# Product of probabilities and values once for four query tiles in forgetting attention and once for two in dilated attention, with pools split by stage

## The chip, the core and the metric

The kernel runs on one core of one Trainium2 chip. The metric is the device time of one execution in microseconds (us). The core has five engines that run at the same time, each through a stream of its own in order: TensorE (PE; its weight loads are listed as PEld), VectorE (DVE), ScalarE (ACT), GpSimd (POOL) and SyncE (SP), which issues the DMAs. TensorE writes to PSUM, which is cut into banks of 512 fp32 columns; the other engines copy from there to SBUF.

## The reference

Two blocks, one after the other, on 1024 tokens of 1024 channels, all in fp32. The first runs a state space model (SSD) and forgetting attention with 16 heads side by side, and merges them; the second runs differential attention with 4 heads and dilated attention with 8, and a gated embedding. The two attentions that the change touches, cut down:

```python
def forgetting_attention(q, k, v, logf):      # 16 heads of 64, 16 + 1024 keys
    c = cumsum(logf)
    for each block of 128 queries i:
        s = q_i @ k.T * scale + (c_i - c_k)
        s = where(kpos <= qpos, s, -inf)      # causal
        p = softmax(s)
        o_i = p @ v

def dilated_attention(q, k, v, slopes):       # 8 heads of 64, three patterns
    for window, dilation in ((128, 1), (512, 4), (2048, 16)):
        # query t sees t + j * dilation, |j| <= window // (2 * dilation)
        o, lse = banded softmax(q @ k.T * scale - slope * distance) @ v
    out = sum(softmax(lse) * o)
```

## The kernel before

All work is written out in one order by hand; no scheduler changes it. A stage is a Python generator that gives back the TensorE time which it has just used by its own estimate, and `merge(a, b, ratio)` takes steps from two of them in turn, so that projections (fp32 split into a high and a low part, three matmuls each, `mm3`, L112 to L114) stand between the steps of an attention. In forgetting attention these steps are also those of the convolution and of the next pair's projections.

Heads go in pairs of two, p = 0 to 7 in forgetting attention, n = 4 to 7 in dilated attention. A pair's 1024 queries are 8 tiles of 128, and `pipeline` (L526) runs three stages over them, the scores two tiles ahead: for tile i the order is A(i+2), C(i-1), B(i).

- A: scores of a tile for both heads (L566, L567, L569 forgetting, L1262 and L1264 dilated) into PSUM; VectorE adds the bias and takes the minimum (L570, L1267; four such reductions for a dilated tile); ScalarE takes the exponential (L573, L1270) into `N`.
- B: the probabilities are transposed on TensorE, 128 x 128 at a time (L620, L1289, L1295), and copied from PSUM to `pt` (L626 on ScalarE in forgetting attention; VectorE and ScalarE in turn in the dilated). In the dilated one 3 x 16 more keys of each head are first gathered by VectorE into `more` (L1285) and transposed by L1296.
- C: the product with the values, 64 output rows per head, both heads in one bank O (L599; L1313). Each is a matmul of 128 query columns, once per block of keys. In forgetting attention L604 adds the first 16 keys of four tiles at once, in the dilated one L1314 adds the `more` keys of a tile.

After every fourth tile O is read out (L606 on VectorE; L1317 on ScalarE). In pairs 4 to 6 of the dilated attention projections of the next pair stand between the steps, with the sums of squares of q and k (L255, transposed by tokens at L264) and a reciprocal root on VectorE (L239 to L246), whose rows are transposed by L271. The last pair, n = 7, has no such work beside it.

Tiles come from a pool `big` of 41 slots (N, pt, projections, weights), from small pools, and from `ph`, which holds what one phase needs (`cb`, `pm`, `E`, the tables). A tile is free again when its last reader is through, and what writes to it next waits for that.

Of the kernel before, what the change touches and what calls it, by code (L numbers as in the profile page):

```python
# [57 lines left out]
# steps of a pair's projections, for the first pair, the differential and the dilated ones: t the tail of the attention  # L58
# before it, f and e what is left to finish of the pairs before it, q, v and z the projections of q, v and the gate,
# N the norms of k and q, x the values by tokens  # L60
# [6 lines left out]
class Kern:  # L67
    def __init__(self, ctx, tc, t, out):
        self.tc, self.nc, self.t, self.out = tc, tc.nc, t, out
        self.big = ctx.enter_context(tc.tile_pool(name="big", bufs=41))  # L70
        self.cst = ctx.enter_context(tc.tile_pool(name="cst", bufs=1))
        self.sm = ctx.enter_context(tc.tile_pool(name="sm", bufs=2))
        self.dr = ctx.enter_context(tc.tile_pool(name="dr", bufs=1, space=bass.MemoryType.DRAM))
        self.ctx, self.psx = ctx, None
        self.psum(8, 0)
        self.n = 0
        self.halfs = None

# [5 lines left out]
    def half(self, name):  # L84
        """512 columns; in the tail from a pool of their own"""
        if self.halfs is None:
            return self.slot(name, w=512)
        return self.halfs.tile([128, 512], F32, tag="half", name=name, bufs=11)

    def psum(self, one, two):  # L90
        """the banks of PSUM from here on: single ones and pairs"""
# [40 lines left out]
    # weight strips, in the order in which they are used  # L132
# [85 lines left out]
    def rstd(self, out, ss, n):  # L218
        """1 / sqrt(ss / n + eps)"""
# [9 lines left out]
    def rsqrt(self, v, pool):  # L229
        """v [128, n] > 0 in place to 1/sqrt(v): a first guess from the exponent, three Newton steps"""  # L230
# [29 lines left out]
    def token_sums_T(self, t, n):  # L260
        """the sums by tokens: [128 tokens, block of 128, part, 32]"""
# [5 lines left out]
    def rows_out(self, v, n, dst):  # L267
        """v [128 tokens, n = (row, block of 128)]: rows of 1024 tokens in DRAM"""
# [56 lines left out]
    def softplus(self, x):  # L325
        """x [128, 9, n] in place to max(x, 0) + log(1 + exp(-|x|)), the logarithm by the series of artanh"""
# [16 lines left out]
    def dt_f(self):  # L343
# [21 lines left out]
        # cumulative log forget gates (negated: csp), as rows  # L365
# [31 lines left out]
    def dt_ssd(self):  # L397
        """SSD: within-chunk cumulative a*dt, decays"""
# [61 lines left out]
    def v_tokens(self, vT, blocks):  # L460
        """vT [128 channels, tokens] -> [128 tokens, block, 128 channels]"""
# [54 lines left out]
    def silu2(self, ps, out):  # L516
        """2 * silu"""
# [5 lines left out]
    def pipeline(n, A, B, C, pre=lambda i: None):  # L523
        """stages of each of n query tiles, the scores two tiles ahead"""
# [13 lines left out]
    def fox_attend(self, p, st):  # L538
# [10 lines left out]
        Ns, PTs, O, M = {}, {}, [None], [None, None]  # L549
# [30 lines left out]
        def B(i):  # L580
            PTs[i] = []
            if i % 4 == 3:
                ps = self.bank()
                te.transpose(ps[:, :128], M[i // 4][:, 0], self.ident)
                nc.vector.tensor_copy(out=M[i // 4][:, 1], in_=ps[:, :128])
            for j in range(2):
                pt = self.slot("pt", w=1024)
                self.transposes(Ns[i][j], 16, i + 1, pt, act=True)
                PTs[i].append(pt)
# [3 lines left out]
        def C(i):  # L593
            if i % 4 == 0:
                O[0] = self.bank()
            for b in range(i + 1):
                for j in range(2):
                    o = O[0][64 * j:64 * j + 64, (i % 4) * 128:(i % 4 + 1) * 128]
                    te.matmul(o, st["v"][:, b, 64 * j:64 * j + 64], PTs[i][j][:, b * 128:(b + 1) * 128],  # L599
                              start=i % 4 == 0 and b == 0, stop=False)  # L600
            del PTs[i]
            if i % 4 == 3:
                for t in range(4):
                    te.matmul(O[0][:, t * 128:(t + 1) * 128], st["vm"][:, t], M[i // 4][:, 1], start=False, stop=t == 3)  # L604
                c = slice((i - 3) * 128, (i + 1) * 128)
                nc.vector.scalar_tensor_tensor(out=y[:, c], in0=O[0], scalar=0.5, in1=st["zs"][:, c], op0=ALU.mult,  # L606
                                               op1=ALU.mult)
            return (i + 1) * 269
# [4 lines left out]
    def transposes(self, N, off, nb, pt, act=False):  # L613
        nc = self.nc
        for g in range(0, nb, 4):
# [5 lines left out]
            self.evac(pt[:, g * 128:(g + n) * 128], ps[:, :n * 128], act)  # L621
# [9 lines left out]
    def conv_strip(self, j):  # L631
        """strip j of xbc: projection, causal convolution, silu; channel-major, all 1040 tokens"""
# [24 lines left out]
    def ssd_chunks(self, g, st):  # L657
# [9 lines left out]
        def tokens(c, c0, w):  # L667
            """x*dt, decayed x*dt and B by tokens"""
# [32 lines left out]
        def prep(c):  # L701
# [9 lines left out]
            E = self.ph.tile([128, 520], F32, tag="cb", name="E", bufs=2)  # L711
# [61 lines left out]
    def ssd_gate(self, g, st):  # L773
        """y * silu(z), the group's sum of squares, out to DRAM"""
# [14 lines left out]
    def ssd_ssq(self, g, st):  # L789
        """1/rms of the group, as a row in DRAM"""  # L790
# [18 lines left out]
    def inv_rows(self, n, dst):  # L809
        """1/l of n heads, as rows in DRAM"""  # L810
# [6 lines left out]
    def gates(self, ms):  # L817
        """tanh(half the gate's argument), out to DRAM"""
# [10 lines left out]
    def load_y(self, g):  # L829
        """four row blocks of the attention's (g < 2) or the SSD's output, hi and lo; the loads run ahead"""  # L830
# [41 lines left out]
    def merge_out(self, ys, late):  # L872
        nc, V, G, t = self.nc, self.nc.vector, self.nc.gpsimd, self.t
        A = [self.slot("A", w=T) for _ in range(8)]
# [95 lines left out]
    def wide_product(self, w, act, wo, begun=(), before=None):  # L970
        """token-major products of act (channel-major halves) with w [1024, 1024]; yields
        (half, token tile of the half, column half, psum); begun: the first sums"""
# [21 lines left out]
    def wide_rows(self, w, ch, out, pool=False, vector=False):  # L994
        """the row blocks of w [K, 1024], columns ch*512.., hi and lo, into out"""
# [13 lines left out]
    def qk_norms(self, parts, dst):  # L1009
        """parts: k and q, each (x, x squared, gain); x * gain / rms of each head of 64; dst: two rows in DRAM  # L1010
        for each"""
# [19 lines left out]
    def raw_project(self, key, st):  # L1031
        """a strip of two heads, and its squares"""
# [769 lines left out]
```

## Time and profile before

| | |
|---|---|
| Time, median of 3 runs | 2734.22 us (2733.99 to 2737.39) |
| Span of the profiled execution | 2737.4 us, as long as the highest time |
| TensorE, matmuls | 2670.8 us busy, 98% |
| VectorE | 1377.0 us, 50% |
| ScalarE | 1171.9 us, 43% |
| GpSimd | 685.0 us, 25% |
| Mean granted clock of TensorE | 0.994 |

The profile is of one execution. Forgetting attention runs from 97 to 682 us, the SSD and the merge after it, the dilated pairs from about 2215 to 2523 us. An engine's busy time is what its instructions took; where an engine was idle, the row names what ended the wait. A matmul's end is modelled, so what a matmul costs is read from the start of one to the start of the next.

### The profile page before, as it was taken

How to read it: one execution, taken by the hardware profiler on the slowest of the kernel's cores; microseconds unless marked ns; L12 is line 12 of the kernel's file. 1: busy time of each engine (PE TensorE's matmuls, PEld its weight loads, DVE VectorE, ACT ScalarE, POOL GpSimd, SP SyncE). 2: the span in 40 equal slices, each digit the busy share in tenths (PEclk: the TensorE clock that was granted, in tenths of full speed). 3: DMA queues.
4: the chain of work that ended last, by engine and by line, in shares of the span. 5: the costliest groups of instructions: out<-in, count | busy, mean ns of one | idle time of the engine just before them, and what ended most of it. 6: DMA issues, size and time to landing. Idle time of an engine off the chain costs nothing. (4 is left out here: it accounts for less than half of the span.)

```text
span 2737.4 us, 40266 instructions
## 1 busy us (share of the span) xinstructions
PE 2670.8 (98%) x15693; PEld 2264.5 (83%) x15693; DVE 1377.0 (50%) x2761; ACT 1171.9 (43%) x2080; POOL 685.0 (25%) x764
## 2 busy tenths in 40 slices
PE   8999999999999999999999999999999999998999
PEld 6888888889989989889887887877878877787887
DVE  5433222333474574664756777445644555446332
ACT  5444444454343443434432113445544554445331
POOL 1111111111244243342433334111111121114321
PEclk9999999999999999999999999999999999999999
DMA  3212222211123123122157654340222223324422
GB/s 124 65 57 78 71 78 78 78 47 47 70 83 118 47 85 116 49 84 108 62 186 253 215 185 161 108 130 26 85 62 78 79 79 97 98 72 138 166 67 70
DMA packets 85471, 266.98 MB, mean 98 GB/s; under 512 B 10880, under 2 KB 12032, under 8 KB 84256
## 3 DMA queue, kind: packets, MB, share of 16 engines
q1 hardware_dynamic: 85280, 264.40, 29.9%
q8 instruction: 123, 2.02, 0.3%
q14 instruction: 68, 0.56, 0.1%
HBM read 205.57 MB, written 33.49 MB: 87 GB/s over the span
## 5 line engine op out<-in xcount | busy, mean ns | idle before, releaser
L121 POOL TENSOR_TENSOR wlo<-wraw,whi 128x1024 fp32r<-128x1024 f32 (+2 forms) x168 | 374.3, 2231 | 1279.5 <-ACT whi L120 1242.6
L112 PE MATMUL bank<-uh,whi 128*128 128x512 f32 (+4 forms) x1752 | 628.4, 359 | 0.1
L114 PE MATMUL bank<-uh,wlo 128*128 128x512 f32 (+4 forms) x1752 | 619.7, 354 | 0.4 <-POOL wlo L121 0.4
L113 PE MATMUL bank<-ul,whi 128*128 128x512 f32 (+4 forms) x1752 | 619.5, 354 | 0.0
L112 PEld LDWEIGHTS bank<-uh,whi 128*128 128x128 f32 (+1 forms) x1752 | 328.9, 188 | 36.4 <-issue 3.5
L114 PEld LDWEIGHTS bank<-uh,wlo 128*128 128x128 f32 (+1 forms) x1752 | 328.6, 188 | 35.9 <-POOL wlo L121 0.9
L113 PEld LDWEIGHTS bank<-ul,whi 128*128 128x128 f32 (+1 forms) x1752 | 328.9, 188 | 32.2
L112 PE MATMUL bank<-u,whi 128*128 128x512 f32 x512 | 207.6, 405 | 0.7 <-ACT pr L931 0.7
L113 PE MATMUL bank<-u,whi 128*128 128x512 f32 x512 | 203.5, 397 | 0.0
L114 PE MATMUL bank<-u,wlo 128*128 128x512 f32 x512 | 203.2, 397 | 0.0
L120 ACT ACTIVATE whi<-wraw 128x1024 fp32r<-128x1024 f32 (+2 forms) x169 | 155.6, 927 | 24.3 <-DMA wraw<-in_w_pa_dram 15.1
L626 ACT ACTIVATE pt<-bank 128x512 f32<-128x512 f32 (+1 forms) x320 | 143.4, 507 | 37.2 <-PE bank L620 28.0
L114 PE MATMUL bank<-yh,wlo 128*128 128x512 f32 x384 | 153.0, 399 | 2.0 <-POOL wlo L121 1.9
L112 PE MATMUL bank<-yh,whi 128*128 128x512 f32 x384 | 152.8, 398 | 1.0 <-ACT whi L120 1.0
L113 PE MATMUL bank<-yl,whi 128*128 128x512 f32 x384 | 152.1, 396 | 0.0
L643 DVE SCALAR_TENSOR_TENSOR acc<-raw,cwh,acc 128x1040 f32<-128x1040 f32 x72 | 93.7, 1302 | 114.0 <-ACT acc L640 112.3
L573 ACT ACTIVATE N<-N,mn 128x272 f32<-128x272 f32 (+7 forms) x128 | 100.6, 786 | 54.3 <-DVE mn L570 51.8
L114 PEld LDWEIGHTS bank<-u,wlo 128*128 128x128 f32 x512 | 97.3, 190 | 23.0
L112 PEld LDWEIGHTS bank<-u,whi 128*128 128x128 f32 x512 | 97.6, 191 | 22.1 <-ACT pr L931 1.1
L113 PEld LDWEIGHTS bank<-u,whi 128*128 128x128 f32 x512 | 97.6, 191 | 20.6
L121 POOL TENSOR_TENSOR wo<-wl,wo 128x512 fp32r<-128x512 f32 x52 | 75.1, 1456 | 156.8 <-ACT wo L120 116.5
L620 PE MATMUL bank<-cm,N 128*128 128x128 f32 x832 | 108.2, 275 | 0.0
(326 smaller groups left out, 4997.5 us busy)
## 6 DMA issues: line engine op xcount, KB each, us to landing
wraw<-in_w_in_dram SPq DMA_DIRECT2D x120, 512.0 KB, 4.6
gt<-d_gate SPq DMA_DIRECT2D x48, 512.0 KB, 4.8
ab<-d_acs SPq DMA_DIRECT2D x32, 512.0 KB, 3.6
qs<-qt SPq DMA_DIRECT2D x48, 256.0 KB, 3.0
wl<-in_w_out_dram SPq DMA_DIRECT2D x48, 256.0 KB, 4.1
tab<-in_tab_dram SPq DMA_DIRECT2D x8, 1056.0 KB, 5.6
cb<-d_csp SPq DMA_DIRECT2D x16, 520.0 KB, 6.1
d_gate<-gt SPq DMA_DIRECT2D x16, 512.0 KB, 2.9
```

Source lines behind the costliest of these rows:

```text
L112: te.matmul(ps, lh, rh, start=start, stop=False)
L113: te.matmul(ps, lh, rl, start=False, stop=False)
L114: te.matmul(ps, ll, rh, start=False, stop=stop)
L120: self.nc.scalar.activation(out=hi, in_=src, func=AF.Copy)
L121: (self.nc.vector if vector else self.nc.gpsimd).tensor_tensor(out=lo, in0=src, in1=hi.bitcast(F32), op=ALU.subtract)
L573: nc.scalar.activation(out=N[:, :W], in_=N[:, :W], func=AF.Exp, scale=-1.0, bias=mn[:, n - 1:n], accum_out=self.lall[:, 2 * p + j, i:i + 1])
L620: nc.tensor.transpose(ps[:, b * 128:(b + 1) * 128], N[:, c:c + 128], self.ident)
L626: self.nc.scalar.activation(out=out, in_=ps, func=AF.Copy)
L643: V.scalar_tensor_tensor(out=acc[:, :L], in0=raw[:, k:k + L], scalar=w(k), in1=acc[:, :L], op0=ALU.mult, op1=ALU.add)
```

## The change

In forgetting attention C does nothing for three tiles of four; at the fourth it runs the product of four tiles with all their keys, up to 512 query columns in one matmul (512, 384, 256, 128 at the diagonal). Its operand is `pt` of shape [128, 4 key blocks, 512 queries], from four buffers of the phase's pool. In the dilated attention C runs for two tiles at every second one, with the matmuls unchanged, first those of L1313 of both tiles, then the two of L1314. The pool `big` has 40 slots, and `ph` is closed and opened again between stages, with pools for forgetting attention, for the SSD (`ph2`), for the merge (`pha`, eight tiles A) and for the second block (`ph3`). Comments and docstrings are gone, so line numbers after the change differ by a few. The estimates that `merge` works by follow: C gives back 0 for the tiles without a product.

```diff
-        self.big = ctx.enter_context(tc.tile_pool(name="big", bufs=41))
+        self.big = ctx.enter_context(tc.tile_pool(name="big", bufs=40))
...
         def B(i):
-            PTs[i] = []
             if i % 4 == 3:
                 ps = self.bank()
                 te.transpose(ps[:, :128], M[i // 4][:, 0], self.ident)
                 nc.vector.tensor_copy(out=M[i // 4][:, 1], in_=ps[:, :128])
+            if i % 4 == 0:
+                PTs[i // 4] = [[self.ph.tile([128, 4, 512], F32, tag="pt", name="pt", bufs=4) for _ in range(2)]
+                               for _ in range(i // 4 + 1)]
+            q = slice((i % 4) * 128, (i % 4 + 1) * 128)
             for j in range(2):
-                pt = self.slot("pt", w=1024)
-                self.transposes(Ns[i][j], 16, i + 1, pt, act=True)
-                PTs[i].append(pt)
+                self.transposes(Ns[i][j], 16, i + 1, [pt[j][:, :, q] for pt in PTs[i // 4]], act=True)
             del Ns[i]
             return 2 * (i + 1) * 109
 
         def C(i):
-            if i % 4 == 0:
-                O[0] = self.bank()
+            if i % 4 != 3:
+                return 0
+            g = i // 4
+            pt = PTs.pop(g)
+            O = self.bank()
             for b in range(i + 1):
+                c0 = max(0, b - 4 * g) * 128
                 for j in range(2):
-                    o = O[0][64 * j:64 * j + 64, (i % 4) * 128:(i % 4 + 1) * 128]
-                    te.matmul(o, st["v"][:, b, 64 * j:64 * j + 64], PTs[i][j][:, b * 128:(b + 1) * 128],
-                              start=i % 4 == 0 and b == 0, stop=False)
...
+                    te.matmul(O[64 * j:64 * j + 64, c0:], st["v"][:, b, 64 * j:64 * j + 64],
+                              pt[b // 4][j][:, b % 4, c0:], start=b == 0, stop=False)
...
-            return (i + 1) * 269
+            return (2.5 + 4 * g) * 910
...
# dilated attention
+        NB = 2
...
-            big, small = self.slot("pt", w=1024), self.slot("pt", w=512)
+            big = self.ph.tile([128, 1024], F32, tag="ptb", name="ptb", bufs=NB)
+            small = self.ph.tile([128, 384], F32, tag="pts", name="pts", bufs=NB)
...
         def C(i):
-            d = dil_tile(i)
-            big, small = PTs.pop(i)
-            if i % 4 == 0:
+            if i % NB != NB - 1:
+                return 0
+            if i % 4 < NB:
                 O[0] = self.bank()
...
-            return 5 * 269 + 216
+            return NB * (5 * 269 + 216)
...
-        A = [self.slot("A", w=T) for _ in range(8)]
+        A = [self.ph.tile([128, T], F32, tag="A", name="A", bufs=8) for _ in range(8)]
```

Where this puts the instructions, at three places. First, forgetting attention, a pair's TensorE from the end of the scores of tile 5 to the transposes of tile 4; N_911 and N_924 are the probabilities of tile 3, pt_1065 and pt_1072 those of tile 3 transposed. Before:

```order
L569 MATMUL bank<-maskb,identb 128x128
L599 MATMUL bank<-pt_1018,vtok_796 64x128
L599 MATMUL bank<-pt_1024,vtok_796 64x128
...
L584 MATMUL bank<-cm,pm 128x128
L620 MATMUL bank<-cm,N_911 128x128 x4
L620 MATMUL bank<-cm,N_924 128x128 x4
...
L599 MATMUL bank<-pt_1065,vtok_796 64x128
L599 MATMUL bank<-pt_1072,vtok_796 64x128
...
L604 MATMUL bank<-pm,vm_789 128x128 x4
L620 MATMUL bank<-cm,N_988 128x128 x5
```

The same place after:

```order
L569 MATMUL bank<-maskb,identb 128x128
L583 MATMUL bank<-cm,pm 128x128
L624 MATMUL bank<-cm,N_911 128x128 x4
L624 MATMUL bank<-cm,N_924 128x128 x4
...
L604 MATMUL bank<-pt,vtok_796 64x512 x2
L604 MATMUL bank<-pt,vtok_796 64x384 x2
L604 MATMUL bank<-pt,vtok_796 64x256 x2
L604 MATMUL bank<-pt,vtok_796 64x128 x2
L607 MATMUL bank<-pm,vm_789 128x128 x4
L624 MATMUL bank<-cm,N_983 128x128 x5
```

The product of tile 2 is gone from between the scores of tile 5 and the transposes of tile 3, and one wide product stands where that of tile 3 stood, behind the scores of tile 6 (not shown).

Second, dilated pair 6, TensorE from the last scores of tile 3 to the end of the transposes of tile 1. Before:

```order
L1264 MATMUL bank<-qt_20890,qs_20918 128x288
L1313 MATMUL bank<-pt_21127,vtok_20987 64x128 x8
L1313 MATMUL bank<-pt_21128,vtok_20987 64x128 x2
L1314 MATMUL bank<-pt_21128,vx_21114 128x128
L1289 MATMUL bank<-cm,N_21070 128x128 x4
L1289 MATMUL bank<-cm,N_21081 128x128 x4
L1295 MATMUL bank<-cm,N_21070 128x128
L1295 MATMUL bank<-cm,N_21081 128x128
L1296 MATMUL bank<-cm,more 96x128
```

The same place after:

```order
L1270 MATMUL bank<-qt_20434,qs_20462 128x288
L1296 MATMUL bank<-cm,N_20614 128x128 x4
L1296 MATMUL bank<-cm,N_20625 128x128 x4
L1302 MATMUL bank<-cm,N_20614 128x128
L1302 MATMUL bank<-cm,N_20625 128x128
L1303 MATMUL bank<-cm,more 96x128
```

The product of tile 0 is gone from here; it stands with that of tile 1 behind the scores of tile 4. L1303 is the line that was L1296.

Third, the same pair, TensorE from the sums of squares to the transpose of the rows of reciprocal roots. Before:

```order
L264 MATMUL bank<-cm,sums_21558 128x128 x4
L1313 MATMUL bank<-pt_21560,vtok_20987 64x128 x8
L1313 MATMUL bank<-pt_21561,vtok_20987 64x128 x2
L1314 MATMUL bank<-pt_21561,vx_21114 128x128
L112 MATMUL bank<-u_1247_15873,whi_21482 128x512
...
L114 MATMUL bank<-u_1250_15876,wlo_21483 128x512
L271 MATMUL bank<-cm,rsv 32x128
```

The same place after:

```order
L264 MATMUL bank<-cm,sums_21102 128x128 x4
L112 MATMUL bank<-u_1111_15416,whi_21014 128x512
...
L114 MATMUL bank<-u_1114_15419,wlo_21015 128x512
L271 MATMUL bank<-cm,rsv 32x128
```

The product of tile 6 has moved behind L271, to that of tile 7.

## Rows read from the trace of the kernel before

**Rows 1.** The page's first part: busy us, share of the span, instructions.

```profile
PE 2670.8 (98%) x15693; PEld 2264.5 (83%) x15693; DVE 1377.0 (50%) x2761; ACT 1171.9 (43%) x2080; POOL 685.0 (25%) x764
```

**Rows 2.** Windows: stretch, length, busy PE, PEld, DVE, ACT, POOL, clock, DMA share, GB/s.

```profile
562.30:579.60 17.30, 17.30 (x154) 14.76 (x154) 11.85 (x39) 11.88 (x26) 1.38 (x7) 1.00 0.08 31
2403.00:2429.40 26.40, 26.25 (x230) 23.21 (x231) 18.11 (x63) 15.44 (x32) 0.00 (x0) 1.00 0.21 67
```

**Rows 3.** Groups by line: busy us, mean ns | idle before, its releaser.

```profile
L599 PE MATMUL bank<-pt,vtok 128*64 128x128 f32 x1152 | 78.5, 278 | 0.0
L1296 PE MATMUL bank<-cm,more 128*96 128x128 f32 x32 | 9.0, 280 | 9.8 <-DVE more L1285 9.8
```

**Rows 4.** Timeline, TensorE: start, us, what; products of tiles 3 and 7.

```profile
571.62 0.23 PE L569 MATMUL bank<-maskb,identb 128*128 128x128 bf16 x1
571.78 1.09 PE L599 MATMUL bank<-pt,vtok 128*64 128x128 f32 x16
572.80 1.16 PE L604 MATMUL bank<-pm,vm 128*128 128x128 f32 x8
...
613.10 1.97 PE L599 MATMUL bank<-pt,vtok 128*64 128x128 f32 x32
615.00 1.16 PE L604 MATMUL bank<-pm,vm 128*128 128x128 f32 x8
```

**Rows 5.** Timeline, TensorE, passes of 512 columns on 32 output rows.

```profile
1940.14 1.05 PE L255 MATMUL bank<-rb,w 128*32 128x512 f32 x4
1941.13 0.50 PE L1167 MATMUL bank<-qs,qs 128*128 128x512 f32 x1
```

**Rows 6.** Timeline, ScalarE, before the product of tile 3.

```profile
569.31 0.95 ACT L573 ACTIVATE N<-N,mn 128x784 f32<-128x784 f32 x1 [0.22 <-DVE mn L570]
570.26 1.06 ACT L626 ACTIVATE pt<-bank 128x512 f32<-128x512 f32 x2
```

**Rows 7.** Timeline, TensorE, products of tiles 0, 1 and 2, each with its successor.

```profile
562.40 0.44 PE L599 MATMUL bank<-pt,vtok 128*64 128x128 f32 x4
562.77 0.66 PE L620 MATMUL bank<-cm,N 128*128 128x128 f32 x4
...
564.75 0.66 PE L599 MATMUL bank<-pt,vtok 128*64 128x128 f32 x8
565.34 0.88 PE L620 MATMUL bank<-cm,N 128*128 128x128 f32 x6
...
567.78 1.08 PE L599 MATMUL bank<-pt,vtok 128*64 128x128 f32 x12
568.79 0.33 PE L584 MATMUL bank<-cm,pm 128*128 128x128 f32 x1
```

**Rows 8.** Timeline, TensorE, dilated pair 6, tiles 0 and 1.

```profile
2403.14 0.32 PE L1296 MATMUL bank<-cm,more 128*96 128x128 f32 x1 [1.98 <-DVE more L1285]
...
2404.65 1.31 PE L1313 MATMUL bank<-pt,vtok 128*64 128x128 f32 x20
...
2406.22 1.04 PE L1289 MATMUL bank<-cm,N 128*128 128x128 f32 x8
...
2407.31 0.27 PE L1296 MATMUL bank<-cm,more 128*96 128x128 f32 x1
```

**Rows 9.** Timeline, VectorE, the copies of tile 1.

```profile
2406.49 0.31 DVE L1285 COPY more<-N 128x48 f32<-128x48 f32 x2
```

**Rows 10.** Timeline, TensorE, sums and rows of the reciprocal roots.

```profile
2447.41 0.60 PE L264 MATMUL bank<-cm,sums 128*128 128x128 f32 x4
...
2453.31 0.28 PE L271 MATMUL bank<-cm,rsv 128*32 128x128 f32 x1 [0.77 <-DVE rsv L246]
```

**Rows 11.** Windows, dilated pairs 5 and 7.

```profile
2296.00:2352.00 56.00, 50.67 (x341) 43.53 (x340) 29.45 (x96) 28.80 (x59) 11.63 (x20) 0.94 0.32 105
2476.00:2523.00 47.00, 37.45 (x344) 32.85 (x342) 32.06 (x103) 28.75 (x62) 25.21 (x23) 0.96 0.39 119
```

**Rows 12.** Groups by line, ScalarE, the decay's reads of `ab`.

```profile
L714 ACT ACTIVATE E<-ab 64x512 f32<-64x512 f32 x64 | 40.1, 626 | 25.5 <-DMA ab<-d_acs 13.5 <-DVE th L752 11.6
```

More of the change, by code (lines that the diff above doesn't have):

```diff
@@ L548, in fox_attend @@
         y = self.slot("y", w=T)
-        Ns, PTs, O, M = {}, {}, [None], [None, None]
+        Ns, PTs, M = {}, {}, [None, None]
         def A(i):
@@ L593, in C, with transposes @@
         def C(i):
-            if i % 4 == 0:
-                O[0] = self.bank()
+            if i % 4 != 3:
[3 more added lines that the diff above has]
+            O = self.bank()
             for b in range(i + 1):
+                c0 = max(0, b - 4 * g) * 128
                 for j in range(2):
-                    o = O[0][64 * j:64 * j + 64, (i % 4) * 128:(i % 4 + 1) * 128]
-                    te.matmul(o, st["v"][:, b, 64 * j:64 * j + 64], PTs[i][j][:, b * 128:(b + 1) * 128],
-                              start=i % 4 == 0 and b == 0, stop=False)
[L601 to L607, printed above, removed]
-            return (i + 1) * 269
+                    te.matmul(O[64 * j:64 * j + 64, c0:], st["v"][:, b, 64 * j:64 * j + 64],
+                              pt[b // 4][j][:, b % 4, c0:], start=b == 0, stop=False)
+            for t in range(4):
+                te.matmul(O[:, t * 128:(t + 1) * 128], st["vm"][:, t], M[g][:, 1], start=False, stop=t == 3)
+            c = slice((i - 3) * 128, (i + 1) * 128)
+            nc.vector.scalar_tensor_tensor(out=y[:, c], in0=O, scalar=0.5, in1=st["zs"][:, c], op0=ALU.mult,
+                                           op1=ALU.mult)
+            return (2.5 + 4 * g) * 910
         yield from self.pipeline(8, A, B, C)
         nc.sync.dma_start(out=self.d_yatt[p], in_=y)
-    def transposes(self, N, off, nb, pt, act=False):
+    def transposes(self, N, off, nb, pts, act=False):
         nc = self.nc
@@ L620, in transposes @@
                 nc.tensor.transpose(ps[:, b * 128:(b + 1) * 128], N[:, c:c + 128], self.ident)
-            self.evac(pt[:, g * 128:(g + n) * 128], ps[:, :n * 128], act)
+            self.evac(pts[g // 4][:, :n], ps[:, :n * 128].rearrange("p (b c) -> p b c", c=128), act)
     def evac(self, out, ps, act=False):
@@ L710, in prep @@
             V.tensor_tensor(out=cbm, in0=self.U, in1=ps[:, :128], op=ALU.mult)
-            E = self.ph.tile([128, 520], F32, tag="cb", name="E", bufs=2)
+            E = self.ph.tile([128, 520], F32, tag="E", name="E", bufs=2)
             for e in range(2):
@@ L1196, in B @@
             pt = self.slot("pt", w=1024)
-            self.transposes(P[0], 0, 8, pt, act=True)
+            r = pt.rearrange("p (b c) -> p b c", c=128)
+            self.transposes(P[0], 0, 8, [r[:, :4], r[:, 4:]], act=True)
             PTs[i] = pt
@@ L1303, in C @@
         def C(i):
-            d = dil_tile(i)
-            big, small = PTs.pop(i)
-            if i % 4 == 0:
+            if i % NB != NB - 1:
+                return 0
+            if i % 4 < NB:
                 O[0] = self.bank()
-            q = slice((i % 4) * 128, (i % 4 + 1) * 128)
-            for b in range(5):
-                for j in range(2):
-                    c = slice(64 * j, 64 * j + 64)
-                    x = big[:, j * 512 + b * 128:j * 512 + (b + 1) * 128] if b < 4 else small[:, j * 128:(j + 1) * 128]
-                    te.matmul(O[0][c, q], st["v"][:, d["blocks"][b][0], c], x, start=b == 0, stop=False)
-            te.matmul(O[0][:, q], st["vx"][:96, i * 128:(i + 1) * 128], small[:96, 256:384], start=False, stop=True)
+            tiles = [(t, dil_tile(t)["blocks"], *PTs.pop(t)) for t in range(i - NB + 1, i + 1)]
+            for t, blocks, big, small in tiles:
+                q = slice((t % 4) * 128, (t % 4 + 1) * 128)
+                for b in range(5):
+                    for j in range(2):
+                        c = slice(64 * j, 64 * j + 64)
+                        x = (big[:, j * 512 + b * 128:j * 512 + (b + 1) * 128] if b < 4
+                             else small[:, j * 128:(j + 1) * 128])
+                        te.matmul(O[0][c, q], st["v"][:, blocks[b][0], c], x, start=t % 4 == 0 and b == 0, stop=False)
+            for t, _, _, small in tiles:
+                te.matmul(O[0][:, (t % 4) * 128:(t % 4 + 1) * 128], st["vx"][:96, t * 128:(t + 1) * 128],
+                          small[:96, 256:384], start=False, stop=t % 4 == 3)
             if i % 4 == 3:
@@ L1543, in build @@
             st = nx
+        phx.close()
+        phx = ExitStack()
+        self.ph = phx.enter_context(self.tc.tile_pool(name="ph2", bufs=1))
         for g in range(4):
@@ L1565, in build @@
         phx.close()
+        phx = ExitStack()
+        self.ph = phx.enter_context(self.tc.tile_pool(name="pha", bufs=1))
         MARK("merge")
@@ L1570, in build @@
         self.psum(4, 2)
+        phx.close()
         phx = ExitStack()
@@ L1787 @@
     from concourse.bass_utils import run_bass_kernel_spmd as _run
-    nc = _bacc.Bacc("TRN2", target_bir_lowering=False, num_devices=1)
+    nc = _bacc.Bacc("TRN2", target_bir_lowering=False, num_devices=1,
+                    dynamic_dma_scratch_size=1024)
     data = layout(inputs)
```

## The prediction

> **What bounds the kernel now.** I read the page's busy shares first: TensorE is busy 98% of the span, VectorE half, ScalarE less [rows 1]. So the time is the length of TensorE's instruction stream plus the few places where it waits, and an edit is worth what it takes off that stream less the waits that it opens. Then the windows by stage: in forgetting attention TensorE is busy 17.30 of 17.30 us, and VectorE and ScalarE do about 11.9 us each in the same stretch, 69% of it; in the middle of a dilated pair TensorE is busy 26.25 of 26.40 us, with VectorE at 18.11 [rows 2]. No engine but TensorE is full, but the others are not so idle that work ordered closer to its consumer would find its operand ready. Third, the groups of TensorE by line, for the number of passes and for the waits that exist: the product L599 waits for nothing, and the small transpose L1296 has waited 9.8 us in 32 for the copies on VectorE [rows 3]. Last, the timelines around each product, for what stands between it and what it reads.
>
> **Forgetting attention, the product.** Per pair it is 1152 / 8 = 144 passes (each fp32 matmul is two) [rows 3]. Between starts, 16 passes took 1.02 us and 32 took 1.90 [rows 4]: 0.055 us a pass and 0.14 fixed. At the sides of a group some 0.19 more is lost: the 128-column bf16 matmul before it takes 0.16 to the next start [rows 4], about three times the 0.055 of a pass of the same columns. I take 0.33 per group, 0.14 being the low end. Now there are 8 groups per pair: 144 x 0.055 + 8 x 0.33 = 10.5 us. After the change two groups remain, with the same columns in wider passes. The nearest row with 512 columns on part of the array is L255: four passes in 0.99 us [rows 5], 0.99 less 0.14, by 4, is 0.21 us, so 0.41 ns per column against 0.055 / 128 = 0.43. The 18,432 columns of all passes cost 7.6 us, and with 2 x 0.33 the pair costs 8.2. So 2.3 us a pair less; with 0.14 per group, 1.1. I take 2.1, near the upper, since 0.14 leaves out both sides of a group.
>
> The wait that it opens is at the first product of a pair, which comes after tile 3. It reads the transposed tiles 0 to 3, and the last of them is copied by ScalarE behind the exponentials of tile 5: the second of these ran from 569.31 to 570.26, the copies to 571.32, and the product began at 571.78, 0.46 later [rows 4, 6]. The products of tiles 0, 1 and 2 stood ahead and are gone: 0.37 + 0.59 + 1.01 = 1.97 us by starts [rows 7], so that TensorE arrives about 2 us earlier, while ScalarE can come at most the 0.22 us earlier that it now waits for VectorE [rows 6]. The wait is then 2.0 - 0.46, less up to 0.22: 1.3 to 1.55; the bounds are 0 (if ScalarE came as much earlier as TensorE) and 2.0. I take 1.5, near the upper, because ScalarE's two rows stand end to end. Behind the waiting product stand the product of the meta keys and the transposes of tile 4, which only TensorE delays. The second product (tiles 4 to 7) has two blocks of projections between the last transposes and itself, and needs nothing later than they give: no wait. Sum per pair: -2.1 + 1.5 = -0.6; eight pairs, **-5 us** (bounds -2.3 x 8 = -18 and (-1.1 + 2.0) x 8 = +7).
>
> **Dilated attention, the product.** A product took from 2404.65 to 2406.22, 1.57 us, for 20 and 2 passes [rows 8]. Two tiles in one step save one group's fixed cost, at 0.33 us four times a pair (bounds 0.14 and 0.42, the last if the change of shape to the one with 96 rows also counts); in three pairs with side work, -4 us.
>
> But the product of the tile before stood between the scores of tile i+2 and the transposes of tile i, and for i = 1, 3, 5 there is nothing in its place. The last transpose, L1296, reads `more`, which VectorE copies behind the four reductions of tile i+2's scores. Now it ends at 2406.49 + 0.31 = 2406.80 and L1296 starts at 2407.31 [rows 8, 9]: 0.51 in hand. VectorE's order is unchanged, and its reductions start from the scores, which do not move. With 1.57 us of cover gone, TensorE waits 1.06 us; nothing else can run, since the scores of the next tile stand behind it. In tile 0, where no product has ever stood ahead, the same wait shows: 1.98 us [rows 8]. Nine such tiles in three pairs cost 9.5 us (bounds 0, if VectorE came earlier by that much, and 9 x 1.57 = 14).
>
> The third place is between the sums L264 and the row transpose L271. There TensorE already waits 0.77 us for VectorE's chain of the reciprocal root, with the product of tile 6 and a block of projections as cover [rows 10]. The product goes behind it: 1.57 us more wait in each of three pairs, +4.7 (bounds 0 and +5). So -4 + 9.5 + 4.7, **+10.2 us**. In the last pair there is no side work, TensorE is busy 37.45 of 47.00 us and VectorE and ScalarE set the pace [rows 11]; four fixed costs less, and about as much in waits that end elsewhere: -1 (bounds -3 and +4).
>
> **Pools.** One slot less in the common pool and phase pools of their own leave the instruction count of ScalarE, VectorE, GpSimd and the DMA queue as it was. A load into a slot waits for a later reader. The nearest row is the decay's read of `ab`, which has waited 13.5 us for its loads in 64 [rows 12]; the others run well ahead. I take +0.5 (bounds 0 and +3).
>
> **Clock.** In dilated pairs the granted clock is already 0.94 and 0.96 on average where TensorE waits [rows 11], so a part of each stretch ran at the lower of the two levels, 1.2 GHz. In the first of these windows that is 0.06 x 56 = 3.4 us of lost columns. New waits of 1 to 2.4 us may bring more such stretches; I put +1.5 (bounds 0 and +10, three more windows like the first).
>
> The sum is -5 + 10.2 - 1 + 0.5 + 1.5 = +6.2, from the profiled span of 2737.4 us to 2743.6. That span is equal to the highest of the three times and 3.2 above their median of 2734.22, so on the median the forecast is **2740.4 us**.
>
> **Rivals.**
> *The new waits of the dilated pairs don't come.* If VectorE starts each tile's reductions earlier, because the double step leaves it time to catch up, +9.5 and +4.7 fall away: -5 - 4 - 1 + 0.5 = -9.5, 2725 us. For it: VectorE is busy 18.11 of 26.40 us. Against: the reductions follow the scores, and these follow the waiting transpose. It decides where `more` ends over 1.5 us ahead of L1296 instead of 0.5. This is the case on the other side.
> *The wait in forgetting attention doesn't come.* ScalarE would have to gain 1.5 us by tile 3: then -18 instead of -5, a net of -7, 2727 us. Against: ScalarE's rows stand end to end there.
> *The clock falls at the new waits.* Then each dilated pair has a window like the first of [rows 11], +10, and forgetting attention, now at 1.00, loses a little too: 2750 to 2756 us. By the Trainium skill, "TensorE: Matmul & The Clock Gate", section "HAM oscillation — how this bites in real kernels", repeated idle stretches between groups of matmuls set the clock back to half each time; by that rule this case would be the likely one. In the trace forgetting attention, where TensorE does not wait, has 1.00, and the middle of pair 6, where it waits 0.15 us in all, 1.00 too [rows 2], so the rule agrees with where the low clock is, but no row shows waits as short as 1 us bringing it.
> *The two heads' passes of 512 columns don't run side by side.* Then the 18,432 columns cost twice as much, 7.6 us more in eight pairs: +61, 2800 us. L255 speaks against it, but its passes use 32 columns of the array and not 64.
>
> **How the numbers follow.** Forecast 0.50, with a range of its own of 2735 to 2748; no dilated waits 0.13; no wait in forgetting attention 0.15; clock 0.19; not side by side 0.03. No change means within 0.2%, 5.5 us, about what a measurement of this kernel can tell: 2728.7 to 2739.7. Faster: all of the second case and half of the third (0.20). Same: the other half and four tenths of the forecast (0.28). Slower: the rest (0.52). The range leaves out the 2800 and the ends of the outer cases: 2724 to 2756.
>
> **What would show it right or wrong.** In forgetting attention the first wide product waits for ScalarE's copies by 1.5 us in each pair, sixteen groups in place of 64, and the busy time of the product falls by about 2 us a pair. In dilated pairs 4 to 6 L1296 waits for VectorE about 1 us in tiles 1, 3 and 5, and L271 2.3 us instead of 0.8. I am wrong if these waits are under half as long, if the wide passes take more than 0.3 us each, or if the granted clock of forgetting attention falls below 0.97.

## The result, and the profile after

The changed kernel takes 2749.91 us, median of 4 runs (2747.4 to 2751.58), against 2735.8 for the kernel before in as many: a ratio of 1.0052, 95% interval 1.0038 to 1.0066. It is slower by 14 us; 2740.4 were forecast. Its profiled execution spans 2748.8 us, so the two traces stand 11.4 us apart and the medians 14.1. The reason is that a run's time is some 1.8 us longer than its span (2750.6 for this profiled run): the span of 2737.4 us before belongs to an execution slower than all four timed ones, of 2738.01 at most.

The page's first part, to be held against [rows 1]:

```profile
PE 2656.5 (97%) x14925; PEld 2231.2 (81%) x14925; DVE 1371.6 (50%) x2761; ACT 1166.9 (42%) x2080; POOL 683.6 (25%) x764
```

TensorE has 14.3 us less to do and the span is longer: it waits more. Where, the start of the same matmul in both traces tells:

| TensorE starts | before | after | difference |
|---|---|---|---|
| first score of forgetting attention | 79.03 | 76.98 | -2.1 |
| first decay product of the SSD | 747.77 | 738.95 | -8.8 |
| first score of dilated pair 4 | 2205.90 | 2197.09 | -8.8 |
| pair 5 | 2298.11 | 2295.51 | -2.6 |
| pair 6 | 2389.06 | 2391.12 | +2.1 |
| pair 7 | 2478.88 | 2487.07 | +8.2 |
| first matmul of the output projection | 2523.22 | 2533.38 | +10.2 |
| last matmul | 2731.76 | 2743.19 | +11.4 |

The first 2 us come ahead of any changed product. A window there shows why, in the kernel before and then after (stretch, length, busy us and instructions of PE, PEld, DVE, ACT, POOL, granted clock, DMA share, GB/s):

```profile
64.00:68.00 4.00, 4.00 (x18) 4.00 (x17) 3.21 (x7) 1.91 (x3) 1.08 (x1) 0.58 0.43 94
```

```profile
60.00:70.00 10.00, 8.78 (x55) 8.15 (x54) 8.20 (x20) 3.30 (x5) 3.53 (x7) 1.00 0.39 105
```

That execution of before ran a piece of its start at the lower clock, the other did not. Of the nine variants further down two have such a piece and seven don't, so it comes and goes between executions; the change has no part in it. Forgetting attention then gains 6.7 us: 662.0 us instead of 668.7 from its first score to the first decay product. From there to dilated pair 4 nothing changes on balance, the dilated pairs lose 19.0 us, 17.0 of them in pairs 4 to 6, and what follows them loses 1.3. (Scores stand ahead of the first product of a stage, so these starts are earlier than the 97 and 2215 us given above.)

The groups of TensorE by line (busy us, mean ns, then idle us before them with the releaser) are those of [rows 3] under new line numbers, and the row transpose of [rows 10]:

```profile
L604 PE MATMUL bank<-pt,vtok 128*64 128x512 f32 (+3 forms) x384 | 69.3, 490 | 5.6 <-ACT pt L630 5.6
L1303 PE MATMUL bank<-cm,more 128*96 128x128 f32 x32 | 9.4, 294 | 22.3 <-DVE more L1292 22.3
L271 PE MATMUL bank<-cm,rsv 128*32 128x128 f32 (+1 forms) x12 | 3.6, 303 | 15.1 <-DVE rsv L246 14.5 <-DVE ld L1193 0.6
```

The first has 5.6 us of waiting where there was none. The second went from 9.8 to 22.3. The third had 9.7 before:

```profile
L271 PE MATMUL bank<-cm,rsv 128*32 128x128 f32 (+1 forms) x12 | 3.3, 275 | 9.7 <-DVE rsv L246 9.2 <-DVE ld L1189 0.6
```

Forgetting attention after, TensorE at the first wide product of pair 6, then the second (start, us, what):

```profile
562.22 0.23 PE L569 MATMUL bank<-maskb,identb 128*128 128x128 bf16 x1
563.21 2.85 PE L604 MATMUL bank<-pt,vtok 128*64 128x512 f32 x16 [0.76 <-ACT pt L630]
565.99 1.16 PE L607 MATMUL bank<-pm,vm 128*128 128x128 f32 x8
...
591.96 5.81 PE L604 MATMUL bank<-pt,vtok 128*64 128x512 f32 x32
597.69 1.05 PE L607 MATMUL bank<-pm,vm 128*128 128x128 f32 x7
```

ScalarE ahead of it:

```profile
561.64 0.94 ACT L573 ACTIVATE N<-N,mn 128x784 f32<-128x784 f32 x1
562.57 1.07 ACT L630 ACTIVATE pt<-bank 128x512 f32<-128x512 f32 x2
```

The copies follow the exponential of tile 5 without a gap, as in [rows 6]; the 0.22 us of waiting for VectorE is gone. The first product starts at 563.21, when the first of the two copies is there; the second ends at 563.64. The group takes 2.78 us to the next start. VectorE's first reduction of tile 5, before and then after:

```profile
566.61 0.56 DVE L570 CUSTOM_DVE_ANT_0 N<-cb,bank 128x392 f32<-128x392 f32 x1 [0.40 <-PE bank L567]
```

```profile
558.94 0.56 DVE L570 CUSTOM_DVE_ANT_0 N<-cb,bank 128x392 f32<-128x392 f32 x1
```

It had waited 0.40 us for TensorE's scores and waits no more: the products that went from ahead of the scores let the scores come earlier, so VectorE moved up, and ScalarE with it.

Dilated pair 6 after, TensorE: tiles 0 and 1, the small transposes of tiles 3 and 5, and the row transpose:

```profile
2405.23 0.32 PE L1303 MATMUL bank<-cm,more 128*96 128x128 f32 x1 [1.97 <-DVE more L1292]
...
2406.64 1.03 PE L1296 MATMUL bank<-cm,N 128*128 128x128 f32 x8
...
2408.88 0.31 PE L1303 MATMUL bank<-cm,more 128*96 128x128 f32 x1 [0.99 <-DVE more L1292]
...
2421.09 0.31 PE L1303 MATMUL bank<-cm,more 128*96 128x128 f32 x1 [1.31 <-DVE more L1292]
...
2433.05 0.31 PE L1303 MATMUL bank<-cm,more 128*96 128x128 f32 x1 [1.04 <-DVE more L1292]
...
2452.47 0.60 PE L264 MATMUL bank<-cm,sums 128*128 128x128 f32 x4
...
2458.43 0.39 PE L271 MATMUL bank<-cm,rsv 128*32 128x128 f32 x1 [2.58 <-DVE rsv L246]
```

VectorE before tile 1's small transpose:

```profile
2408.08 0.52 DVE L1273 CUSTOM_DVE_ANT_0 N<-tab,bank,mn 128x288 f32<-128x288 f32 x1
...
2408.52 0.31 DVE L1292 COPY more<-N 128x48 f32<-128x48 f32 x2
```

The last of the four reductions stands right ahead of the copies, the copies end at 2408.83, and TensorE goes on at 2408.88. In [rows 8] the product filled this place and the transpose came 0.5 us after the copies.

The clock, by the windows of the four dilated pairs, before and after:

```profile
2205.90:2298.10 92.20, 86.69 (x558) 71.22 (x559) 46.58 (x129) 45.49 (x76) 16.28 (x35) 0.96 0.28 87
2298.10:2389.10 91.00, 84.82 (x551) 70.43 (x551) 46.98 (x124) 44.54 (x76) 14.10 (x22) 0.96 0.29 88
2389.10:2478.90 89.80, 83.48 (x551) 69.33 (x551) 46.90 (x124) 43.76 (x74) 19.16 (x38) 0.98 0.28 84
2478.90:2540.00 61.10, 53.69 (x411) 46.16 (x412) 34.04 (x107) 36.23 (x74) 33.15 (x30) 0.97 0.54 172
```

```profile
2197.10:2295.50 98.40, 87.87 (x558) 72.39 (x559) 46.15 (x129) 44.90 (x76) 16.17 (x35) 0.95 0.26 81
2295.50:2391.10 95.60, 84.27 (x550) 70.46 (x551) 46.59 (x124) 44.58 (x76) 14.12 (x22) 0.96 0.29 84
2391.10:2487.10 96.00, 84.28 (x551) 70.46 (x551) 46.99 (x124) 43.64 (x74) 19.27 (x38) 0.96 0.26 79
2487.10:2551.40 64.30, 54.99 (x416) 48.23 (x417) 33.93 (x107) 36.70 (x74) 34.93 (x31) 0.95 0.54 171
```

What is missing to 1.00, times the length, is an estimate of the time lost (too high where TensorE waits): 11 us before and 16 after, 5 us more. The plainest part of it stands right behind the row transposes. From each of them to the next small transpose, in pairs 4, 5 and 6, after and then before:

```profile
2267.30:2272.70 5.40, 5.40 (x23) 4.46 (x24) 0.14 (x2) 1.12 (x3) 0.00 (x0) 0.70 0.32 93
2362.80:2368.30 5.50, 5.50 (x24) 4.56 (x25) 0.18 (x3) 1.19 (x3) 0.00 (x0) 0.70 0.41 96
2458.40:2463.90 5.50, 5.47 (x23) 4.53 (x24) 0.21 (x3) 1.15 (x3) 0.00 (x0) 0.70 0.06 20
```

```profile
2272.70:2276.70 4.00, 4.00 (x25) 3.42 (x25) 0.18 (x3) 1.20 (x3) 0.00 (x0) 1.00 0.17 49
2363.50:2367.50 4.00, 3.97 (x23) 3.40 (x24) 0.19 (x2) 1.13 (x3) 0.00 (x0) 1.00 0.15 55
2453.30:2457.30 4.00, 3.99 (x23) 3.43 (x24) 0.19 (x3) 1.10 (x3) 0.00 (x0) 1.00 0.04 8
```

The same matmuls take 5.5 us instead of 4.0, because a part of them ran at the lower level. Each of the three waits of 2.6 us is thus followed by another 1.5 us of loss, 4.5 in all. The other differences about cancel: the first 9 us of pair 5 have 0.81 where they had 0.62, and some 10 us in the middle of pair 7 have 0.82 where they had 1.00.

### The profile page after: what moved, and what is told of

It is laid out like the page before. It is cut to its first block, busy times and chain, and to the rows that moved or that the text cites. A ratio compares the mean times of both kernels' runs of the same rounds, so it can differ in the third digit from the quotient of the medians.

```text
span 2748.8 us, 38652 instructions
## 1 busy us (share of the span) xinstructions
PE 2656.5 (97%) x14925; PEld 2231.2 (81%) x14925; DVE 1371.6 (50%) x2761; ACT 1166.9 (42%) x2080; POOL 683.6 (25%) x764
## 5 line engine op out<-in xcount | busy, mean ns | idle before, releaser
L630 ACT ACTIVATE pt<-bank 128x512 f32<-128x512 f32 (+3 forms) x256 | 114.0, 515 | 38.4 <-PE bank L624 38.0
```

Of the source, the lines that this page charges most:

```text
L630: self.nc.scalar.activation(out=out, in_=ps, func=AF.Copy)
```

## The experiments

The theories: (1) the whole loss is made in the dilated pairs, where the product, moved to every second tile, no longer covers two waits for VectorE; forgetting attention gains and the pools cost nothing. (2) Rival: the lost slot and the split pools, or the pace of VectorE and ScalarE as such, make part of it. All of the kernels are variants of the changed one. Like it they are built with `dynamic_dma_scratch_size=1024`, which the kernel before is not and which the text on the change leaves out; whatever that does is counted with the pools. "Before" was timed beside each and lay at 2735 to 2737 us.

**The dilated product once per tile again.**

```diff
-        NB = 2
+        NB = 1
...
-            big = self.ph.tile([128, 1024], F32, tag="ptb", name="ptb", bufs=NB)
+            big = self.ph.tile([128, 1024], F32, tag="ptb", name="ptb", bufs=2)
...
```

> The changed kernel with the dilated product once per tile again (its two buffers and the split pools stay). Theory (the loss is made in the dilated pairs, by the waits that the double step opens; forgetting attention gains 0.8 us a pair and the pools cost nothing): 2729 us, 0.998 of before, with the wait for the gathered keys back at about 10 us in 32. Rival (the pools or the lost slot make part of the loss): 2735 or more.

Measured: 2731.94 us, ratio 0.9981 (0.9972 to 0.9991). The small transpose and the row transpose wait about as long as before, where it was 9.8 and 9.7 us:

```profile
L1303 PE MATMUL bank<-cm,more 128*96 128x128 f32 x32 | 9.0, 282 | 8.9 <-DVE more L1292 8.9
L271 PE MATMUL bank<-cm,rsv 128*32 128x128 f32 (+1 forms) x12 | 3.3, 276 | 9.9 <-DVE rsv L246 9.3 <-DVE ld L1193 0.6
```

Three us over the forecast, but faster than before: the wide product of forgetting attention and the pools together gain 4.6 us (by the interval 2.5 to 7.7, which holds the 6.7 of the traces; forgetting attention takes 662.0 us in this trace too), and the double step is what loses 18.

**The product of forgetting attention once per tile again.**

```diff
+            for b in range(i + 1):
+                for j in range(2):
+                    te.matmul(O[64 * j:64 * j + 64, (i % 4) * 128:(i % 4 + 1) * 128], st["v"][:, b, 64 * j:64 * j + 64],
+                              PTs[i][j][:, b], start=i % 4 == 0 and b == 0, stop=False)
...
             if i % 4 != 3:
-                return 0
...
+                return (i + 1) * 269
```

> The changed kernel with the product of forgetting attention once per query tile again, its transposed probabilities in common slots; the dilated double step and the split pools stay. Theory (the parts add): 2756 us, 1.007 of before, 6 to 7 above the changed kernel. Rival (part of the loss in the dilated pairs comes from forgetting attention's share of the pool or from where the stage starts): 2745 to 2750.

Measured: 2754.83 us, ratio 1.0065 (1.005 to 1.008). The waits of the dilated pairs are those of the changed kernel, 21.7 and 15.2 us, and forgetting attention takes 668.1 us, 668.7 before. The double step with the pools loses 18.3 us, the wide product with the pools gains 4.6, both together lose 14.1: by the medians the parts add within 0.4 us. The pools are counted in both parts, so they make no more than that by the medians; the intervals leave 3 to 4 us either way on each number.

**VectorE's copies of the gathered keys ahead of the reductions.** They are issued at the head of A(i+2) instead of in B(i).

```diff
         def A(i):
+            if i > 1:
+                gather(i - 2)
             d = dil_tile(i)
```

> The changed kernel with VectorE's copies of the gathered keys of tile i ahead of the four reductions of tile i+2 instead of behind them. Theory (TensorE waits only because these two copies are queued behind reductions that need its own new scores): the wait of 22 us in 32 falls under 4, and with fewer stretches at the lower clock the time to 2728, range 2724 to 2733. Rival (VectorE's and ScalarE's work per tile sets the pace of a tile, and the wait only moves to the scores' banks or to the copies of the transposes): 2743 or more.

Measured: 2739.34 us, 10.6 under the changed kernel, ratio to before 1.0006 (0.9997 to 1.0015).

```profile
L1315 PE MATMUL bank<-cm,more 128*96 128x128 f32 x32 | 8.9, 279 | 0.4 <-DVE more L1266 0.4
L1335 PE MATMUL bank<-ptb,vtok 128*64 128x128 f32 x512 | 34.7, 276 | 3.3 <-ACT ptb L630 2.4 <-DVE ptb L632 0.5
L1284 PE MATMUL bank<-qs,qs 128*128 128x288 f32 (+1 forms) x64 | 23.0, 360 | 1.5 <-DVE mn L1287 1.2
```

The wait is gone, 22.3 to 0.4 us, so its cause was the place of these copies in VectorE's queue. The time missed its range of 2724 to 2733 and lies short of the rival's 2743: 4.8 us of waiting came up again at the product's operands and the scores' banks, as the rival had it, and the runs were spread widely (2734 to 2743). The trace is that of the fastest of the ten. Its span of 2732.7 us is 16.1 under the changed kernel's, about what 21.9 us of waiting less and 4.8 more would give; what made the median run 5 us slower than this one isn't shown.

**Tiles 6 and 7 one at a time.**

```diff
-            if i % NB != NB - 1:
+            n = 1 if i > 5 else NB
+            if i % n != n - 1:
                 return 0
```

> The changed kernel with the products of dilated tiles 6 and 7 one at a time, so that tile 6's again stands between the sums of squares and the transpose of the reciprocal roots' rows. Theory (this wait is the cover that the product gave, 1.8 us a pair): the wait before that transpose back from 2.6 to 0.8 us, the time 2745, 4 to 5 under the changed kernel. Rival (the wait is set by the chain on VectorE, which starts later for other reasons): 2749 to 2750.

Measured: 2741.99 us, 7.9 under the changed kernel, where 4 to 5 were expected. The row transpose waits 9.9 us again instead of 15.1, 5.2 less, as the theory said, while the wait for the gathered keys is 23.8 us, 1.5 more. The gain is bigger than the two make, and the granted clock tells a part of the rest. Behind the three row transposes it is 1.00 again, and the matmuls up to the next small transpose take 4.0 us. The windows of whole pairs show less plainly what the edit did: pair 4 also lacks lower stretches ahead of the edited place (1.00 up to 2260 us, 0.95 in the changed kernel), and pair 5 has a longer one at its start, both of which the edit doesn't touch:

```profile
2196.70:2290.30 93.60, 83.78 (x558) 68.45 (x559) 46.00 (x129) 44.90 (x76) 16.22 (x35) 1.00 0.28 85
2290.30:2384.10 93.80, 84.25 (x550) 70.18 (x550) 46.58 (x124) 44.54 (x76) 14.08 (x22) 0.96 0.28 86
2384.10:2477.20 93.10, 83.23 (x551) 69.32 (x551) 46.92 (x124) 43.66 (x75) 19.32 (x38) 0.98 0.27 81
```

**Both together, and the single product with the copies ahead.**

> The changed kernel with the copies of the gathered keys ahead and tiles 6 and 7 one at a time. Theory (the two waits are separate and their costs add): 2731 us, 8 under the one with the copies ahead alone, so that the double step as such costs nothing once both waits are gone; against the kernel with single products and copies ahead it would then still be slower by 5 to 10 through the copies of its operands. Rival (one stretch at the lower clock was counted in both): 2736.

> Wide product in forgetting attention, dilated product once per tile, and VectorE's copies of the gathered keys ahead of the next reductions. Theory (the waiting copies cost the kernel before as well, 9 us in tile 0 and the last pair, and lower the clock behind them): 2721 us, 2716 to 2726, about 11 under the same kernel with the copies behind. Rival (VectorE and ScalarE set the pace, the wait moves to the product's operands, as part of it did with the double step): 2727 to 2731.

Measured: 2731.85 us for the double step, 0.9986 (0.9977 to 0.9995), and 2726.37 for the single one, 0.9963 (0.9951 to 0.9976). The two waits add: 7.5 us under the kernel with the copies ahead alone, as one at a time gave 7.9. With both gone the double step is still 5.5 us slower than the single one, so it shows no gain of its own. This difference has no shown cause: the double step's runs had a mean granted clock of 0.992 to 0.997 and the single one's 0.997 to 0.998, and 0.002 of 2730 us is, as an estimate, 5 us. The single one came out between the theory's range and the rival's: of the 8.9 us that it had waited for the copies, 3.7 came back at the product, whose matmuls on `ptb` waited 2.1 us before the edit and 5.8 after it, most of it for ScalarE's copies.

**VectorE copies the transposes of tile 3 in forgetting attention.**

```diff
-                self.transposes(Ns[i][j], 16, i + 1, [pt[j][:, :, q] for pt in PTs[i // 4]], act=True)
+                self.transposes(Ns[i][j], 16, i + 1, [pt[j][:, :, q] for pt in PTs[i // 4]], act=i != 3, dve=i == 3)
...
+            if dve:
+                nc.vector.tensor_copy(out=pts[g // 4][:, :n], in_=src)
+            else:
+                self.evac(pts[g // 4][:, :n], src, act)
```

> The kernel before this one, and in forgetting attention VectorE instead of ScalarE copies the transposes of tile 3, so that the first wide product doesn't stand behind the exponentials of tile 5. Theory (the 0.7 us wait in each of eight pairs, and what the second head waits inside the group, is ScalarE's queue): the wait falls under 0.2 us, the time by 5 to 8 us, to 2715. Rival (the copies delay the reductions of tile 6 on VectorE and the wait moves to the scores): no change within 3 us.

Measured: 2722.13 us, 4.2 under the kernel without it, for 5 to 8 expected; 0.9946 (0.9933 to 0.996). In the traces forgetting attention takes 656.4 us, 5.6 less than without it. TensorE, and VectorE's copies of tile 3:

```profile
558.52 0.23 PE L569 MATMUL bank<-maskb,identb 128*128 128x128 bf16 x1
558.70 2.96 PE L604 MATMUL bank<-pt,vtok 128*64 128x512 f32 x16
561.59 1.16 PE L607 MATMUL bank<-pm,vm 128*128 128x128 f32 x8
```

```profile
557.96 1.28 DVE L627 COPY pt<-bank 128x512 f32<-128x512 f32 x2
```

The group now starts 0.18 us after its predecessor, not 0.99, but it takes 2.89 us, where the 5120 columns of its 16 passes, at 0.41 ns each and with 0.14 fixed, make 2.24. The second copy ends at 559.24, 0.54 us after the group's start. Two more kernels ask whether that is why.

**The meta keys' matmuls ahead of the wide ones.**

```diff
+            for t in range(4):
+                te.matmul(O[:, t * 128:(t + 1) * 128], st["vm"][:, t], M[g][:, 1], start=t == 0, stop=False)
             for b in range(i + 1):
...
-            for t in range(4):
-                te.matmul(O[:, t * 128:(t + 1) * 128], st["vm"][:, t], M[g][:, 1], start=False, stop=t == 3)
```

> Wide product in forgetting attention with the meta keys' four matmuls of full width ahead of the wide ones instead of behind, dilated product once per tile, copies of the gathered keys ahead; ScalarE still copies tile 3. Theory (the first group of 16 passes takes 2.8 us instead of 2.2 because the second head's copy lands half a microsecond after the first head's, so that the heads run out of step and the last pass runs alone; a microsecond of other work ahead covers the wait and puts them in step): the first group 2.3 us, its wait gone, 8 x (0.75 + 0.5) = 10 us under the kernel with the copies ahead alone, 2716. Rival (the length of the first group comes from the unequal widths at the diagonal): group still 2.8 us, only the wait of 0.75 goes: 2720.

> The same with VectorE copying the transposes of tile 3. Theory (heads out of step): the first group, 2.9 us with VectorE's copies and the meta keys behind, falls to 2.3 us, eight times 0.6 = 5 us under that kernel, 2717, level with the kernel in which ScalarE copies. Rival (unequal widths): 2722 as before.

Measured: 2719.99 us with ScalarE's copies, 0.9932 (0.9918 to 0.9945), and 2718.39 with VectorE's, 0.9928 (0.9916 to 0.9941). The first wide group of pair 6 in the second:

```profile
555.92 2.37 PE L606 MATMUL bank<-pt,vtok 128*64 128x512 f32 x16
558.23 0.98 PE L624 MATMUL bank<-cm,N 128*128 128x128 f32 x7
```

2.31 us, as forecast, with the same unequal widths: the length had come from the two heads running out of step, since the second copy lands half a microsecond or more after the first. VectorE's copies in this kernel, and ScalarE's in the other:

```profile
554.25 1.28 DVE L627 COPY pt<-bank 128x512 f32<-128x512 f32 x2
```

```profile
559.46 1.07 ACT L630 ACTIVATE pt<-bank 128x512 f32<-128x512 f32 x2
...
560.42 1.06 ACT L573 ACTIVATE N<-N,mn 128x912 f32<-128x912 f32 x1
```

VectorE's end at 555.53, ahead of the group's start at 555.92. ScalarE's end at 560.53, while that kernel's group starts at 560.23, with the second head late again: it takes 2.66 us, and there the expectation of 2.3 failed; the time of 2719.99 is the rival's 2720, not 2716. Forgetting attention takes 654.5 us with ScalarE's copies and 651.9 with VectorE's. By the times alone the two kernels can't be told apart: the second's runs go from 2715 to 2723. The best version is 19 us faster than the kernel before, and it runs the dilated product once per tile.

## Why the prediction held, and which sizes were off

The sign, the places of the waits and the outer range held; the forecast was +6 and the measurement +14, and the result lies 2 us outside 2735 to 2748, the range given to the forecast alone. On the traces pairs 4 to 6 lose 17.0 us, where 10.2 and most of 1.5 for the clock were forecast; the last pair loses 2.0 instead of gaining 1; the output projection, which has no term, loses 1.3; and forgetting attention gains 1.7 more than forecast, which hides a part of this. By steps:

- *Forgetting attention, -5 forecast, -6.7 measured.* The wait was to be 1.5 us and is 0.76 in pair 6, 5.6 in the eight pairs: just under half as long, which the prediction named as a sign of being wrong. But the rest of it is inside the group. The prediction let the product wait for both copies; TensorE starts with the first head's, and the group then takes 2.78 us instead of 2.24, because the second head runs behind. Together this is 1.3 us, and with it the saving comes out at the 2.1 that were forecast (0.84 gained per pair and 1.3; its lower bound, given as 1.1, is 1.2 by the prediction's own numbers). ScalarE came earlier by more than the 0.22 us of its own wait: VectorE had 0.40 us of idle time for TensorE's scores ahead of tile 5's reductions, which the dropped products gave back, and the whole chain behind moved up. The second group takes 5.73 us to the next start, as 0.41 ns a column would have it (13,312 columns, 5.6). The busy time of the product fell by 1.2 us a pair, not by 2, since the longer first group counts as busy.
- *The small transpose, +9.5 forecast.* L1303's idle time grew by 12.5 us, 9.5 of it in pairs 4 to 6 and 3.0 in the last pair. In tiles 1, 3 and 5 of pair 6 it is 0.99, 1.31 and 1.04 us, for 1.06 forecast; from start to start, which counts the modelled end of the matmul before as well, 1.15, 1.48 and 1.21, and 10.7 in the three pairs. The mechanism is as described and the size right; taking the copies ahead ended the wait.
- *The row transpose, +4.7 forecast, +5.4 measured*, 2.58 us in pair 6. Putting one product back ended it. What the prediction didn't tie to this wait is the clock behind it, another 4.5 us.
- *The last pair, -1 forecast, +2.0 measured* up to the output projection. This step had the wrong sign. The trace of the changed kernel has one wait of 3.17 us for the gathered keys in its tile 3, against 1.8 before, and at its end the row transpose of 1/l waits 1.4 us for VectorE, which it did not before; waits of 2.2 us at the old product are gone. The likely reading, which no run tests, is that where VectorE and ScalarE set the pace a fixed cost saved on TensorE is nothing, and a later product makes what follows it late.
- *Clock, +1.5 forecast, about +5 measured.* The granted clock of the dilated pairs is 0.95 to 0.96 after. The waits of 2.6 us at the row transposes were each followed by the lower level in this trace, and with waits of 0.8 us (before, and with tiles 6 and 7 one at a time) none was. But the variants with the same 2.6 us show it less often: two of three with the dilated product alone changed, one of three with the copies ahead. So such a wait can bring the lower level, but it doesn't do so each time, as the rule cited with the rival on the clock has it. That rival was given 0.19, with 2750 to 2756; the result of 2749.9 lies at its foot, though forgetting attention kept 1.00.
- *Pools, +0.5 forecast:* no cost is seen, but a small one could be hidden. The two traces are as far apart at the first decay product as at dilated pair 4. On the way the changed kernel loses 2 us up to about 1430 us, and gets them back where the profiled execution of before ran at 0.73 and 0.65 (1444 to 1455 us).
- *Double step as such, -4 forecast.* The fixed costs did fall: two products take 2.80 us from start to start (2410.39 to 2413.19 in pair 6) instead of twice 1.57, 0.34 less for 0.33 forecast. But with both waits removed the kernel is slower than with single steps, so this gain is not one that reaches the end.

In pairs 4 to 6, 10.7 us at the small transpose, 5.4 at the row transpose and some 3.5 of clock (4.5 behind the row transposes, less elsewhere) are 19.6; less 4 of fixed costs this is 15.6 of the 17.0, and 1.4 us stay unassigned. That the result still lies inside the outer range is in part luck: what pairs 4 to 6, the last pair and the output projection lose beyond the forecast is hidden in part by what forgetting attention gains beyond it. No run took the last pair alone.

## What to carry to other kernels

On a full engine that executes in order, a block of its work is also the cover for whatever the next instruction reads: before moving it, look for how long ahead that operand is ready now, and compare the margin with the block's length. When a wait is expected to grow, ask how far the waited-for engine moves up too, through its own idle gaps. And before fusing work, put the copies that it reads at the right place in the other queues; with single products that alone was worth 5.6 us (2731.94 to 2726.37), about as much as the wide product's 4.6 to 6.7, while the double step brought no gain in any variant.

## What the runs showed of the hardware that was not expected

Two matmuls of 64 output rows each, one per head, ran side by side only while both had their operands. In step, the second head's first matmul starts 0.01 us after the first head's, and 16 passes take 2.31 us (VectorE's copies, meta keys ahead). With the second head's copy late it starts 0.49 us after it in the changed kernel (563.21 and 563.70) and 0.60 with VectorE's copies alone (558.70 and 559.30), and the passes take 2.78 and 2.89 us: the group is longer by the whole delay, which isn't made up. In the changed kernel's trace each of three waits of about 2.6 us on TensorE was followed by a stretch at the lower clock, so that 4.0 us of matmuls took 5.5; with waits of 0.8 us at the same places none was. Why it doesn't always follow stays open: of six more such waits, in two variants, three were followed by it. Open too is the stretch in the first 70 us, which the change leaves alone: three of the eleven profiles have one there, the others none.
